# Two feed-forwards with seven block products instead of eight

## The chip, the cores and the metric

The kernel runs on one core of a Trainium2 chip, as one launch. What counts is the device time of that launch in microseconds (us). A core has five engines that run their own queues in order: TensorE (PE, matmuls; its weight loads are listed as PEld), VectorE (DVE), ScalarE (ACT), GpSimd (POOL) and SyncE (SP, which here issues DMAs). They meet through semaphores. Operands lie in SBUF, matmul results in PSUM, which has eight banks of 128 x 512 words.

## The reference, cut to what matters

Two models of two layers each run one after the other on 512 tokens of 1024 features in float32. The first model's two layers end in the feed-forward that the change touches:

```python
def _swiglu(h, w_gate, w_up, w_down):
    return (jax.nn.silu(h @ w_gate) * (h @ w_up)) @ w_down
...
    h = h + _swiglu(_rmsnorm(h, norm_ffn[layer]), w_gate[layer], w_up[layer], w_down[layer])
```

`w_gate` and `w_up` are 1024 x 2816, `w_down` is 2816 x 1024. In slices of 128 that is 8 input slices and 22 hidden ones (`KT`, `FT`).

## The kernel before, in words

Activations are kept transposed: features on the 128 partitions, the 512 tokens along the row. A float32 product is made of three matmuls in the fp32r type: each operand is split into a high part (a rounded copy, made by ACT) and a low part (the value less its high part, made by DVE), and `mm3` adds high x high, low x high and high x low in PSUM. Weights are the stationary operand, so each matmul of 512 columns loads another 128 x 128 weight tile.

Weights arrive in blocks of up to 128 x 1024 words (`wst`, one block for one output slice of 128 and up to eight input slices). `plan` lists all blocks in the order of use, and `w_dma` (L242) fetches them through SP into three buffers. `w_hi` (L274) makes a block's high part `whi` on ACT, `w_lo` (L288) its low part `wlo` on DVE; there are three pairs of `whi` and `wlo` in these parts of the kernel. `cols` (L328) runs one block: 24 matmuls into one bank, then `w_done` (L313) frees the pair, starts the high part of the block three ahead, evacuates the bank and makes that block's low part. The program's order on each engine is the order in which the code calls it; nothing reorders it.

`swiglu` (L1009) takes the 22 hidden slices in three chunks (`CHUNKS`: 8, 7, 7). For each slice it runs gate and up over the eight input slices; DVE scales the bank by the norm's factor `r_bc` (L1018, L1026), ACT applies silu (L1019), DVE multiplies (L1027), and `split_act` (L508) makes the high and low parts `hh`, `hl`. Then down adds the chunk to `x`, slice by slice (`add_res`, L770). The first three blocks run before the norm's factor is known (`first_cols`, L353). With the last chunk each finished slice of `x` is also prepared for the next part (`rms_prep`, L529: high and low part, and POOL adds the squares, L527). In these feed-forwards POOL does little else. The second feed-forward is the same code on the second layer.

## Time and profile before

| what | us |
|---|---|
| median of 3 runs (2577.56 to 2585.64) | 2585.27 |
| the profiled execution | 2584.21 |
| its span, first to last instruction | 2582.3 |
| PE busy in the span | 2533.5 |
| DVE busy in the span | 1557.3 |
| POOL busy in the span | 443.6 |

The profile is one execution. A stretch is given as its two ends, counted in us from the span's start. In the rows below, a timeline gives start, duration, engine, line of the kernel, operation, tile written <- tiles read, shapes and how many were merged, with the idle time before it in brackets. A stretch gives its length, then for PE, PEld, DVE, ACT and POOL the busy time with the number of instructions, then the granted clock of PE as a share of full speed (1.00 is 2.4 GHz, half of it 1.2 GHz), the busy share of the DMA engines and GB/s. A group gives its count, busy time and the mean of one in ns, then the idle time before. Durations of matmuls overlap, since PE takes the next while the last one drains; what one matmul costs is read from start to start.

### The profile page before, as it was taken

To read this page: it belongs to the slowest core of one execution; us is meant where nothing else is said; L and a number is where in the kernel's file an instruction comes from. 1 tells how busy PE (TensorE), PEld (TensorE's weight loads), DVE (VectorE), ACT (ScalarE), POOL (GpSimd) and SP (SyncE) were. 2 spreads that over 40 slices of the span, in tenths; PEclk is the share of its full clock that TensorE was granted. 3 is DMA by queue.
4 is the path that set the end of the run, shared out by engine and by line. 5 is a ranking of instruction groups with operands and counts; after the bars stand their busy time and mean duration, and the time that the engine had idled before them with its cause. 6 is when DMAs were issued, how large, how long until landed. Compare 5 with 4: busy or idle time off the path is not lost.

```text
span 2582.3 us, 32942 instructions
## 1 busy us (share of the span) xinstructions
PE 2533.5 (98%) x12732; PEld 2097.1 (81%) x12732; DVE 1557.3 (60%) x2580; ACT 1045.8 (40%) x1736; POOL 443.6 (17%) x394
## 2 busy tenths in 40 slices
PE   9999999999999999999999999999999999999998
PEld 7777888888767788888888888788888777888887
DVE  7665643444767654444476667764556788745556
ACT  6666422223344442222333333443333574534243
POOL 2112100001545210000111124200102326100103
PEclk9999999999989999999999999899999999999998
DMA  4111222232312122222221112232322312232321
GB/s 146 51 49 48 92 98 98 89 102 96 103 58 77 62 96 92 98 98 99 98 95 58 66 37 78 82 113 92 98 97 83 107 50 74 93 103 88 100 93 55
DMA packets 71277, 220.19 MB, mean 85 GB/s; under 512 B 8741, under 2 KB 15013, under 8 KB 71120
## 3 DMA queue, kind: packets, MB, share of 16 engines
q1 hardware_dynamic: 70512, 216.57, 25.5%
q8 instruction: 100, 1.64, 0.3%
q0 software_dynamic: 464, 1.27, 0.2%
q14 instruction: 57, 0.47, 0.1%
q10 hardware_dynamic: 144, 0.25, 0.0%
HBM read 209.14 MB, written 5.24 MB: 83 GB/s over the span
## 4 chain that ended last, share of the span: by engine, by line
PE 88%; DVE 8%; ACT 2%; issue 1%; DMA 0%; SPq 0%; POOL 0%; DVEq 0%; ACTq 0%
PE bank L225 87%; DVE wlo L295 1%; DVE lt L640 1%; DVE pr L1548 1%; PE bank L1165 1%; ACT whi L286 1%; DVE pr L1157 0%; DVE pr L1535 0%; DVE ln_sm L545 0%; DVE hg L1265 0%; PE bank L1558 0%; DVE hq L1342 0%; DVE xl L653 0%; DMA x<-in_xT 0%; DVE sm L1538 0%
## 5 line engine op out<-in xcount | busy, mean ns | idle before, releaser
L286 ACT ACTIVATE whi<-wst 128x1024 fp32r<-128x1024 f32 (+2 forms) x410 | 411.1, 1008 | 936.5 <-PE bank L225 750.1
L225 PE MATMUL bank<-xh,whi 128*128 128x512 f32 (+1 forms) x1992 | 780.9, 392 | 7.3 <-DVE xh L650 4.8
L225 PE MATMUL bank<-xl,whi 128*128 128x512 f32 (+1 forms) x1992 | 773.5, 388 | 5.0 <-DVE xl L653 2.7
L225 PE MATMUL bank<-xh,wlo 128*128 128x512 f32 (+1 forms) x1992 | 770.5, 387 | 2.3 <-DVE wlo L295 2.3
L295 DVE TENSOR_TENSOR wlo<-wst,whi 128x1024 fp32r<-128x1024 f32 (+2 forms) x392 | 486.4, 1246 | 100.9 <-ACT whi L286 97.4
L225 PEld LDWEIGHTS bank<-xh,whi 128*128 128x128 f32 x1992 | 379.9, 191 | 90.3 <-issue 14.8
L225 PEld LDWEIGHTS bank<-xl,whi 128*128 128x128 f32 x1992 | 379.0, 190 | 85.8 <-DVE xl L653 6.8
L225 PEld LDWEIGHTS bank<-xh,wlo 128*128 128x128 f32 x1992 | 379.9, 191 | 74.4 <-DVE wlo L295 3.7
L225 PE MATMUL bank<-hh,whi 128*128 128x512 f32 (+1 forms) x760 | 285.4, 375 | 0.0
L225 PE MATMUL bank<-hl,whi 128*128 128x512 f32 (+1 forms) x760 | 284.2, 374 | 0.0
L225 PE MATMUL bank<-hh,wlo 128*128 128x512 f32 (+1 forms) x760 | 284.2, 374 | 0.0
L527 POOL TENSOR_TENSOR acc<-acc,sq 128x512 f32<-128x512 f32 x35 | 50.0, 1428 | 789.6 <-ACT sq L526 789.2
L770 DVE TENSOR_TENSOR x<-x,bank 128x512 f32<-128x512 f32 x96 | 65.9, 688 | 187.4 <-PE bank L225 187.4
L225 PEld LDWEIGHTS bank<-hh,wlo 128*128 128x128 f32 x760 | 143.2, 188 | 25.7 <-issue 0.5
L225 PEld LDWEIGHTS bank<-hh,whi 128*128 128x128 f32 x760 | 143.2, 188 | 25.7 <-issue 0.5
L225 PEld LDWEIGHTS bank<-hl,whi 128*128 128x128 f32 x760 | 143.2, 188 | 25.2
L574 POOL TENSOR_TENSOR x<-x,r_bc 128x512 f32<-128x512 f32 x32 | 46.5, 1462 | 480.4 <-ACT r_bc L572 419.9
L225 PE MATMUL bank<-whi,xh 128*128 128x256 f32 x416 | 122.0, 293 | 0.0
L225 PE MATMUL bank<-wlo,xh 128*128 128x256 f32 x416 | 119.5, 287 | 0.0
L225 PE MATMUL bank<-whi,xl 128*128 128x256 f32 x416 | 119.5, 287 | 0.0
L1410 DVE SCALAR_TENSOR_TENSOR b<-bank,vecs,b 128x511 f32<-128x511 f32 x88 | 65.9, 749 | 85.8 <-ACT b L1408 84.2
L1410 DVE SCALAR_TENSOR_TENSOR a<-bank,vecs,a 128x511 f32<-128x511 f32 x88 | 65.9, 749 | 83.8 <-ACT a L1408 82.2
(285 smaller groups left out, 3537.2 us busy)
## 6 DMA issues: line engine op xcount, KB each, us to landing
wst<-in_w SPq DMA_DIRECT2D x314, 512.0 KB, 3.2
wst<-in_w SPq DMA_DIRECT2D x64, 448.0 KB, 3.1
wst<-in_w SPq DMA_DIRECT2D x36, 256.0 KB, 2.7
t<-t SPq DMA_DIRECT2D x56, 64.0 KB, 2.0
rel_scratch<-sq SPq DMA_DIRECT2D x16, 192.0 KB, 2.1
x<-in_xT SPq DMA_DIRECT2D x8, 256.0 KB, 6.2
bias<-rel_scratch SPq DMA_DIRECT2D x16, 128.0 KB, 2.9
out_dram<-x SPq DMA_DIRECT2D x16, 128.0 KB, 1.8
```

The source lines that it names most:

```text
L225: self.nc.tensor.matmul(out, lhsT=l, rhs=r, start=start, stop=True, skip_group_check=True)
L286: self.nc.scalar.activation(out=self.split[i][0][:, 0:n], in_=self.staged[i][:, 0:n], func=AF.Copy)
L295: (eng or self.lo_eng or self.nc.vector).tensor_tensor(out=lo[:, 0:n], in0=st[:, 0:n], in1=hi[:, 0:n].bitcast(F32), op=ALU.subtract)
L527: self.defer(lambda: eng.tensor_tensor(out=self.acc, in0=self.acc, in1=sq, op=ALU.add))
L574: nc.gpsimd.tensor_tensor(out=self.x[:, j, :], in0=self.x[:, j, :], in1=self.r_bc, op=ALU.subtract)
L640: nc.vector.scalar_tensor_tensor(out=t, in0=self.x[:, m, cs], scalar=gm, in1=self.acc[:, cs], op0=ALU.mult, op1=ALU.mult)
L770: self.nc.vector.tensor_tensor(out=self.x[:, m, :], in0=self.x[:, m, :], in1=bank, op=ALU.add)
L1165: nc.tensor.transpose(bk[:, P * j:P * j + P], pr[h][:, P * j:P * j + P], self.ident)
L1410: nc.vector.scalar_tensor_tensor(out=t[:, sh:S], in0=bank[:, 0:S - sh], scalar=self.vec(f"cw{l}{tap}", f), in1=t[:, sh:S], op0=ALU.mult, o ...
L1548: nc.vector.tensor_scalar(out=pr[h][:, 0:W], in0=pr[h][:, 0:W], scalar1=sm[:, 4 + h:5 + h], scalar2=None, op0=ALU.mult)
```

## The change

In both feed-forwards the products of gate, up and down are computed on two by two blocks: for a pair of output slices and pairs of input slices, A is the weights' four quarters (output slice by even or odd input slice), B the activations' four (even or odd input slice by half of the tokens). Seven products of sums replace the eight of the plain rule; each has 256 columns (half of the tokens). Gate and up do so for 9 of the 11 pairs of hidden slices; the first two pairs (`PLAIN`) stay as they were. Down does so for all, in chunks of 4, 4 and 3 pairs (`PCHUNKS`).

Left sides: `S1` to `S4` are sums of weight quarters, made on POOL (`s_adds`) when the same sum of the group before has been read; `w_hi` and `w_lo` then split each of the seven left sides in a piece of 512 (384 in the last chunk), two pieces to a pair of buffers. A fourth weight buffer is added. Right sides: `T1` to `T4` are sums of quarters of the activations. For gate and up they are made once per feed-forward from the normalised `x` (`normed`, `sides_a`, `sides_b`, `sides_in_place`) while the plain slices run; for down once for each pair of hidden slices (`make_h`). Out of PSUM come four sums (`b1`, `b6`, `b7`, `b5`); `seven` combines them through `U` and `V`, and `ev_gate`, `ev_up`, `ev_down` finish each quarter. The product of gate and up, and the sum into `x` in the first two chunks, move to POOL. `down` of a chunk runs between gate and up of the next chunk's first pair.

```diff
+PCHUNKS = ((0, 4), (4, 8), (8, 11))
+PLAIN = 2
+
+PIECES = ("S1", "A11", "S3", "S2", "A12", "A22", "S4")
...
+def swiglu_order():
+    out, done = [], None
+    for c in PCHUNKS:
+        for j in range(max(c[0], PLAIN), c[1]):
+            out.append(("gate", j))
+            if done:
+                out.append(("down", done))
+                done = None
+            out.append(("up", j))
+        done = c
+    return out + [("down", done)]
...
+    def group(w, c, k0, n):
+        for m in (2 * c, 2 * c + 1):
+            out.append((w, [(k, m) for b in (0, 1) for k in range(k0 + b, k0 + n, 2)], None, m == 2 * c))
...
-            self.staged[i] = self.ring.tile([P, 1024], F32, name="wst", bufs=3)
+            self.staged[i] = self.stages.pop(0)
...
+            i = self.n_dma - 2
+            if i >= 0 and self.blocks[i][3] and not (i >= 2 and self.blocks[i - 2][3]):
+                self.s_adds(i, ("S1", "S2", "S3", "S4"))
...
+    def s_adds(self, i, names):
+        how = {"S1": ("A21", "A22", ALU.add), "S2": ("S1", "A11", ALU.subtract), "S3": ("A11", "A21", ALU.subtract),
+               "S4": ("A12", "S2", ALU.subtract)}
+        for n in names:
+            a, b, op = how[n]
+            self.nc.gpsimd.tensor_tensor(out=self.side(i, n), in0=self.side(i, a), in1=self.side(i, b), op=op)
...
+            for h, (i, name) in enumerate(load):
+                src = self.side(i, name)
+                c = slice(512 * h, 512 * h + src.shape[-1])
+                self.nc.vector.tensor_tensor(out=lo[:, c], in0=src, in1=hi[:, c].bitcast(F32), op=ALU.subtract)
+                more = i + 2 < len(self.blocks) and self.blocks[i + 2][3]
+                if more and name in ("S1", "S2", "S4"):
+                    self.s_adds(i + 2, {"S1": ("S1",), "S2": ("S2", "S3"), "S4": ("S4",)}[name])
+                if name in ("A12", "A22"):
+                    self.stages.append(self.staged.pop(i + int(name[1]) - 1))
+                    self.w_fetch()
...
+    def seven(self, name, nk, act, banks, evac):
+        x, y = banks
+        b1, b6, b7, b5 = x[:, 0:256], x[:, 256:512], y[:, 0:256], y[:, 256:512]
+        uv = self.uv.tile([P, 2, 256], F32, name="uv", bufs=2)
+        U, V = uv[:, 0, :], uv[:, 1, :]
+        tt = self.nc.vector.tensor_tensor
+        steps = (
+            ("S1", "T1", b5, True, None),
+            ("A11", "B11", b1, True, lambda: self.nc.scalar.activation(out=U, in_=b1, func=AF.Copy)),
+            ("S3", "T3", b7, False, None),
+            ("S2", "T2", b6, False, lambda: (tt(out=U, in0=b6, in1=U, op=ALU.add), tt(out=V, in0=b7, in1=U, op=ALU.add),
+                                             evac(1, 1, b5, V))),
+            ("A12", "B21", b1, False, lambda: evac(0, 0, b1, None)),
+            ("A22", "T4", b7, False, lambda: evac(1, 0, b7, U)),
+            ("S4", "B22", b5, False, lambda: evac(0, 1, b5, U)),
+        )
+        for side, other, out, start, then in steps:
+            load = self.loads[self.wi]
+            i, n = load[self.half]
+            assert n == side and self.blocks[i][0] == name and self.wi < self.n_lo, (load, side, name)
+            hi, lo = (t[:, 512 * self.half:512 * self.half + 512] for t in self.split[self.wi])
+            for k in range(nk):
+                c = slice(k * P, (k + 1) * P)
+                self.mm3(out, hi[:, c], lo[:, c], act(other, 0, k), act(other, 1, k), start and k == 0)
+            self.half += 1
+            full = self.half == len(load)
+            if full:
+                self.half = 0
+                self.wi += 1
+                self.w_free()
+                self.w_hi()
+            if then:
+                then()
+            if full:
+                self.w_lo()
+            self.flush()
...
+            def make_h(j):
+                b11, b12, b21, b22 = b[:, 0, 0:256], b[:, 0, 256:S], b[:, 1, 0:256], b[:, 1, 256:S]
+                rows = (slice(0, 1), slice(1, 3), slice(3, 7))
+                src = (b[:, 0:1, 0:256], b[:, 1, :].rearrange("p (a c) -> p a c", a=2), t4)
+                hi = lambda n: nc.scalar.activation(out=h[j][0][:, rows[n], :], in_=src[n], func=AF.Copy)
+                lo = lambda n: ve(out=h[j][1][:, rows[n], :], in0=src[n], in1=h[j][0][:, rows[n], :].bitcast(F32), op=ALU.subtract)
+                hi(0)
+                hi(1)
+                ve(out=t4[:, 0], in0=b12, in1=b11, op=ALU.subtract)
+                ve(out=t4[:, 2], in0=b22, in1=b12, op=ALU.subtract)
+                ve(out=t4[:, 1], in0=b22, in1=t4[:, 0], op=ALU.subtract)
+                ve(out=t4[:, 3], in0=b21, in1=t4[:, 1], op=ALU.subtract)
+                hi(2)
+                lo(0)
+                lo(1)
+                self.defer(lambda: lo(2))
...
+            def normed(k):
+                v = (even, odd)[k % 2][:, k // 2, :]
+                nc.vector.scalar_tensor_tensor(out=v, in0=self.x[:, k, :], scalar=self.vec(f"norm_ffn{l}", k), in1=self.r_bc,
+                                               op0=ALU.mult, op1=ALU.mult)
+            def side_x(n, src):
+                out = [quad(t[:, n, :, :]) for t in tx]
+                nc.scalar.activation(out=out[0], in_=src, func=AF.Copy)
+                self.defer(lambda: ve(out=out[1], in0=src, in1=out[0].bitcast(F32), op=ALU.subtract))
+            def sides_a():
+                gp(out=t1, in0=quad(x12), in1=quad(x11), op=ALU.subtract)
+                side_x(0, t1)
+                gp(out=t3, in0=quad(x22), in1=quad(x12), op=ALU.subtract)
+                side_x(2, t3)
+            def sides_b():
+                t2 = quad(t4)
+                gp(out=t2, in0=quad(x22), in1=t1, op=ALU.subtract)
+                side_x(1, t2)
                 self.flush()
-
-            def ev_u(i):
-                def f(bank):
-                    b = pool.tile([P, S], F32, name="b", bufs=2)
-                    nc.vector.tensor_tensor(out=b, in0=bank, in1=self.r_bc, op=ALU.mult)
-                    nc.vector.tensor_tensor(out=b, in0=b, in1=hold["a"], op=ALU.mult)
-                    self.split_act(h, i, b)
+                gp(out=t1, in0=quad(x21), in1=t2, op=ALU.subtract)
+                side_x(3, t1)
...
+            def sides_in_place():
+                for m, c, src in ((0, 0, x11), (1, 0, x21), (1, 256, x22)):
+                    hi, lo = (t[:, m:KT:2, c:c + 256] for t in self.xn)
+                    nc.scalar.activation(out=hi, in_=src, func=AF.Copy)
+                    ve(out=lo, in0=src, in1=hi.bitcast(F32), op=ALU.subtract)
+            extra = [lambda k=k: (normed(2 * k), normed(2 * k + 1)) for k in range(4)] + [sides_a, sides_b]
+            names = [(f"{n}{l}", e) for f in range(2 * PLAIN) for n, e in (("gate", ev_g(f % 2)), ("up", ev_u(f)))]
+            run(self.first_cols([n for n, _ in names[:3]], self.xn, [lin.next() for _ in range(3)], [e for _, e in names[:3]]))
+            todo = {3: extra[0:2], 4: extra[2:4], 5: extra[4:5], 6: extra[5:6]}
+            for n, (name, e) in enumerate(names[3:], 3):
+                for f in todo.get(n, ()):
+                    f()
+                run(self.cols(name, range(KT), self.xn, lin.next(), e))
+            self.flush()
+            sides_in_place()
+            pre_cm.__exit__(None, None, None)
+            post_cm = self.tc.tile_pool(name="post", bufs=1)
+            h += sides_of_pairs(post_cm.__enter__(), (2, 3))
...
+            def ev_up(j):
+                def f(m, n, bank, more):
+                    c = slice(256 * n, 256 * n + 256)
+                    if more is None:
+                        ve(out=b[:, m, c], in0=bank, in1=a[:, m, c], op=ALU.mult)
+                        return
+                    ve(out=b[:, m, c], in0=bank, in1=more, op=ALU.add)
+                    if (m, n) == (1, 0):
+                        gp(out=b[:, 1, :], in0=b[:, 1, :], in1=a[:, 1, :], op=ALU.mult)
+                    if (m, n) == (0, 1):
+                        gp(out=b[:, 0, c], in0=b[:, 0, c], in1=a[:, 0, c], op=ALU.mult)
+                        self.defer(lambda: make_h(j))
                 return f
 
...
+                    t = pool.tile([P, 256], F32, name="t", bufs=2)
+                    ve(out=t, in0=bank, in1=more, op=ALU.add)
+                    eng(out=x, in0=x, in1=t, op=ALU.add)
...
+            for what, j in swiglu_order():
+                if what == "gate":
+                    self.seven(f"gate{l}", 4, act_x, pairs.next(), ev_gate)
+                elif what == "up":
+                    self.seven(f"up{l}", 4, act_x, pairs.next(), ev_up(j % 4))
+                else:
+                    self.flush()
+                    for m in range(4):
+                        self.seven(f"down{l}", j[1] - j[0], act_h, pairs.next(), ev_down(m, j is PCHUNKS[-1]))
```

What stands on DVE in the first feed-forward, before: three blocks of weights (`wlo`), each with the evacuation of one bank (`a` gate, `b` up) and its split (`hl`).

```order
L1026 TENSOR_TENSOR b<-bank_73,r_bc 128x512
L1027 TENSOR_TENSOR b<-b,a 128x512
L295 TENSOR_TENSOR wlo_100<-wst,whi_99 128x1024
L1018 TENSOR_TENSOR a<-bank_74,r_bc 128x512
L514 TENSOR_TENSOR hl<-b,hh 128x512
L295 TENSOR_TENSOR wlo_102<-wst,whi_101 128x1024
```

Now, in the second half of one `up` and the start of the next `gate`: `S_2550` to `S_2553` are S1 to S4, `wst` the weight buffers, `t_2549` the four sums T of a pair, `uv` holds U and V.

```order
L382 TENSOR_TENSOR wlo_102<-S_2552,whi_101 128x512
L382 TENSOR_TENSOR wlo_102<-S_2551,whi_101 128x512
L1282 TENSOR_TENSOR b<-bank_79,uv 128x256 x2
L382 TENSOR_TENSOR wlo_98<-wst_2554,whi_97 128x512
L382 TENSOR_TENSOR wlo_98<-wst_105,whi_97 128x512
L1187 TENSOR_TENSOR t_2549<-b 128x256
L1188 TENSOR_TENSOR t_2549<-b 128x256
L1189 TENSOR_TENSOR t_2549<-b,t_2549 128x256
L1190 TENSOR_TENSOR t_2549<-b,t_2549 128x256
L1184 TENSOR_TENSOR hl_2884<-b,hh_2883 128x256
L1184 TENSOR_TENSOR hl_2884<-b,hh_2883 128x512
L1184 TENSOR_TENSOR hl_2884<-t_2549,hh_2883 128x1024
```

Where there was one `wlo` of 1024 for 24 matmuls of 512 columns there are now two of 512 for 24 matmuls of 256, with sums of 256 out of two banks between them and the seven right sides of the pair at its end.

POOL before, around the start of the first feed-forward: the last sums of the attention, then sums of squares (`acc`), most of them from the end of the feed-forward, and the first gain of the next part's weights.

```order
L971 TENSOR_TENSOR spl_2168<-sp,sph_2167 128x256
L971 TENSOR_TENSOR spl_2171<-sp,sph_2170 128x256
L527 TENSOR_TENSOR acc<-acc,sq 128x512 x10
L267 TENSOR_TENSOR wst<-wst,vecs 128x1024
L527 TENSOR_TENSOR acc<-acc,sq 128x512
```

POOL now, in the steady part of gate and up: the four sums of each group's weights, and the product of gate and up in two pieces.

```order
L349 TENSOR_TENSOR S_2550<-wst_104 128x512
L349 TENSOR_TENSOR S_2551<-S_2550,wst_103 128x512
L349 TENSOR_TENSOR S_2552<-wst_103,wst_104 128x512
L1284 TENSOR_TENSOR b<-b,a 128x512
L1286 TENSOR_TENSOR b<-b,a 128x256
L349 TENSOR_TENSOR S_2553<-wst_103,S_2551 128x512
L349 TENSOR_TENSOR S_2550<-wst_105 128x512
L349 TENSOR_TENSOR S_2551<-S_2550,wst_2554 128x512
```

Between two products there are eight sums of 512, where POOL had nothing at all.

DVE before, where slices of gate and up follow each other, as everywhere in the chunk:

```order
L295 TENSOR_TENSOR wlo_98<-wst,whi_97 128x1024
L1018 TENSOR_TENSOR a<-bank_76,r_bc 128x512
L514 TENSOR_TENSOR hl<-b,hh 128x512
L295 TENSOR_TENSOR wlo_100<-wst,whi_99 128x1024
L1026 TENSOR_TENSOR b<-bank_77,r_bc 128x512
L1027 TENSOR_TENSOR b<-b,a 128x512
```

DVE now, from the evacuation of the last plain `up` to the normalised low parts `xl` that the second of the seven products reads:

```order
L1207 TENSOR_TENSOR b<-bank_73,r_bc 128x512
L1208 TENSOR_TENSOR b<-b,a 128x512
L1187 TENSOR_TENSOR t_2549<-b 128x256
L1188 TENSOR_TENSOR t_2549<-b 128x256
L1189 TENSOR_TENSOR t_2549<-b,t_2549 128x256
L1190 TENSOR_TENSOR t_2549<-b,t_2549 128x256
L1184 TENSOR_TENSOR hl_2544<-b,hh_2543 128x256
L1184 TENSOR_TENSOR hl_2544<-b,hh_2543 128x512
L382 TENSOR_TENSOR wlo_100<-wst_2554,whi_99 128x512
L382 TENSOR_TENSOR wlo_100<-wst_105,whi_99 128x512
L1184 TENSOR_TENSOR hl_2544<-t_2549,hh_2543 128x1024
L1249 TENSOR_TENSOR xl<-even,xh 128x4x256
```

The evacuation of the last plain slice, the seven right sides of its pair and two pieces of weights stand ahead of `xl`.

## Rows read from the trace of the kernel before

**Rows 1.** The page, busy time of each engine
```profile
PE 2533.5 (98%) x12732; PEld 2097.1 (81%) x12732; DVE 1557.3 (60%) x2580; ACT 1045.8 (40%) x1736; POOL 443.6 (17%) x394
```

**Rows 2.** The page, chain that ended last, by engine
```profile
PE 88%; DVE 8%; ACT 2%; issue 1%; DMA 0%; SPq 0%; POOL 0%; DVEq 0%; ACTq 0%
```

**Rows 3.** Stretches: both feed-forwards, and one around a pause of PE
```profile
core 0: us, PE busy (x) PEld busy (x) DVE busy (x) ACT busy (x) POOL busy (x), PEclk, DMA share, GB/s
292.50:653.00 360.50, 360.48 (x1598) 298.82 (x1599) 159.95 (x202) 105.00 (x130) 16.59 (x11) 1.00 0.29 96
934.80:1295.00 360.20, 360.17 (x1597) 298.62 (x1598) 160.16 (x202) 105.66 (x130) 10.03 (x7) 1.00 0.29 96
706.00:722.00 16.00, 11.25 (x30) 7.29 (x29) 11.96 (x22) 5.41 (x12) 5.24 (x4) 0.68 0.21 69
```

**Rows 4.** Timeline of PE: start, duration; 512 columns, first feed-forward
```profile
399.91 0.39 PE L225 MATMUL bank<-hh,whi 128*128 128x512 f32 x1
...
410.79 0.39 PE L225 MATMUL bank<-hh,whi 128*128 128x512 f32 x1
```

**Rows 5.** Timeline of PE, 256 columns, each with another weight tile
```profile
206.84 0.28 PE L225 MATMUL bank<-whi,xl 128*128 128x256 f32 x1
...
212.35 0.28 PE L225 MATMUL bank<-wlo,xh 128*128 128x256 f32 x1
```

**Rows 6.** Timeline of DVE and POOL, runs of one instruction merged, at 13 us
```profile
13.57 6.87 DVE L517 SCALAR_TENSOR_TENSOR xl<-x,vecs,xh 128x512 fp32r<-128x512 f32 x4
...
13.48 10.34 POOL L527 TENSOR_TENSOR acc<-acc,sq 128x512 f32<-128x512 f32 x6 [0.39 <-ACT sq L526]
```

**Rows 7.** Timeline of DVE and POOL, two places where both run
```profile
637.45 1.90 POOL L267 TENSOR_TENSOR wst<-wst,vecs 128x1024 f32<-128x1024 f32 x1
...
638.79 0.69 DVE L770 TENSOR_TENSOR x<-x,bank 128x512 f32<-128x512 f32 x1 [2.47 <-PE bank L225]
...
1630.32 0.77 POOL L646 TENSOR_TENSOR x<-lt,acc 128x256 f32<-128x256 f32 x1 [0.95 <-ACT r_bc L641]
...
1630.42 1.75 DVE L295 TENSOR_TENSOR wlo<-wst,whi 128x1024 fp32r<-128x1024 f32 x1
```

**Rows 8.** Timeline of DVE, instructions without a wait between them
```profile
639.39 0.69 DVE L514 TENSOR_TENSOR xl<-x,xh 128x512 fp32r<-128x512 f32 x1
...
1606.82 0.42 DVE L579 TENSOR_TENSOR x<-x,bank 128x256 f32<-128x256 f32 x1 [0.19 <-PE bank L225]
...
1607.16 0.42 DVE L594 TENSOR_TENSOR acc<-acc,sq 128x256 f32<-128x256 f32 x1
```

**Rows 9.** Groups by line, shapes apart: DVE, ACT, POOL; busy us, mean ns
```profile
L295 DVE TENSOR_TENSOR wlo<-wst,whi 128x1024 fp32r<-128x1024 f32 x52 | 63.3, 1221 | 12.7 <-ACT whi L286 12.5
...
L295 DVE TENSOR_TENSOR wlo<-wst,whi 128x512 fp32r<-128x512 f32 x24 | 16.7, 702 | 3.8 <-ACT whi L286 3.7
...
L653 DVE TENSOR_TENSOR xl<-x,xh 128x256 fp32r<-128x256 f32 x48 | 19.5, 417 | 3.2 <-ACT xh L652 3.2
...
L946 DVE TENSOR_TENSOR spl<-sp,sph 128x384 fp32r<-128x384 f32 x32 | 17.9, 559 | 2.1
...
L1276 DVE SCALAR_TENSOR_TENSOR x<-x,vecs,r_bc 128x512 f32<-128x512 f32 x8 | 5.4, 747 | 0.0
...
L579 DVE TENSOR_TENSOR x<-x,bank 128x256 f32<-128x256 f32 x40 | 16.4, 413 | 10.1 <-PE bank L225 8.7 <-POOL acc L591 1.4
...
L286 ACT ACTIVATE whi<-wst 128x1024 fp32r<-128x1024 f32 x314 | 331.0, 1058 | 735.0 <-PE bank L225 579.7 <-issue 142.9 <-POOL wst L267 4.5
...
L286 ACT ACTIVATE whi<-wst 128x512 fp32r<-128x512 f32 x32 | 19.9, 626 | 37.6 <-PE bank L225 34.3 <-issue 2.2 <-ACT pr L1149 1.1
...
L295 POOL TENSOR_TENSOR wlo<-wst,whi 128x1024 fp32r<-128x1024 f32 x10 | 23.9, 2395 | 2.7 <-ACT whi L286 2.5
...
L591 POOL TENSOR_TENSOR acc<-acc,x 128x256 f32<-128x256 f32 x39 | 30.5, 781 | 42.3 <-DVE x L579 35.2 <-DVE ln_sm L545 5.5 <-DVE acc L594 0.7
```

**Rows 10.** The page, DMA issues of weight blocks
```profile
wst<-in_w SPq DMA_DIRECT2D x314, 512.0 KB, 3.2
```

202 lines of the change are left out of this document (144 added, 58 removed).

## Prediction

> **What bounds the kernel now.** I read the shares of busy time first, then the chain that ended last, then the two feed-forwards as stretches, then what VectorE (DVE) and GpSimd (POOL) do to each other, because the change hands both of them work. TensorE (PE) is busy 98% of the span, DVE 60%, POOL 17% [rows 1], and PE carries 88% of the chain [rows 2]. Each of the two feed-forwards is a stretch of 360 us in which PE is busy throughout at full clock, DVE 160 us and POOL 10 to 17 us [rows 3]. So before, PE alone sets the pace there, and the question is whether the change leaves it so.
>
> **What it does to PE.** From one matmul of 512 columns to the next there are 0.2267 us: 48 steps between the two rows of [rows 4]. With 256 columns and a fresh weight tile for each it is 0.1198 us, 46 steps in [rows 5]. Half the columns cost 53% of the time, so seven products cost 7 x 2 x 0.53 / 16 of the eight: most of the eighth is kept. Per feed-forward the change replaces 864 matmuls of gate and up (9 pairs of slices x 96) and 528 of down, 1392 x 0.2267 = 315.6 us, by 9 x 168 + 4 x 11 x 21 = 2436 of 256 columns, 291.8 us. That is 23.8 us less, 47.6 us in both. It is the whole gain.
>
> By the page TensorE: Matmul & The Clock Gate of the Trainium skill (Back-to-back issue gap), a stream of weight load and matmul sustains about 131 ns at 512 columns and about 81 ns at 128; 256 columns then lie between, some 98 ns as an estimate, and 84 x 98 ns against 48 x 131 ns would make seven products dearer than eight. The trace has 227 and 120 ns where the page has 131 and its estimate 98, so I keep the gain.
>
> **What it costs DVE and POOL in steady state.** Take one pair of slices, gate and up: PE needs 168 x 0.1198 = 20.1 us, before 96 x 0.2267 = 21.8.
> DVE issues an instruction 0.61 us after one of 512 the starts at 638.79 and 639.39 in [rows 7, 8], 0.34 after one of 256 [rows 8], 1.14 after one of 1024 (its 1.22 less the same 0.08). Per pair it gets 14 low parts of 512 (8.5 us), 11 sums or products of 256 that read PSUM (3.7), four sums for T1 to T4 each waiting for the one before (4 x 0.42 = 1.7, taken at a full 256-wide duration, [rows 9]) and the low parts of the seven right sides (0.34 + 0.61 + 1.14 = 2.1): 16.0 us, which would fit.
> POOL gets 8 sums of weight quarters of 512 and two products, of 512 and 256. They are not free for DVE. At 13.5 us both had such work queued: six POOL sums took 10.34 us and four DVE instructions 6.87 us, 1.72 us each [rows 6], so they took turns; alone the DVE one takes 0.61, and a POOL 512 thus holds DVE up for 1.11 us. A 1024-wide DVE instruction with 256 of POOL ahead of it took 1.75 instead of 1.22 us [rows 7, 9], so 0.6 for a POOL 256. A DVE instruction with one operand in PSUM is not held: 0.69 us in the middle of a POOL instruction of 1.90 [rows 7].
> So POOL's holds are 9 x 1.11 + 0.6 = 10.6 us a pair. If every one falls on a DVE instruction with both operands in SBUF, the pair takes 16.0 + 10.6 = 26.6 us; if the 3.7 us of PSUM reading always run beneath POOL, 22.9. Either is above PE's 20.1 and above the 21.8 of before: the lower end holds unless POOL's work falls into time in which DVE has nothing to do, and there is none left once DVE is behind. I take 23.4, near the lower end, as both queues are then hardly ever empty, with half a microsecond for DVE's waits on its own results and on POOL's product. Nine pairs: +1.6 x 9 = +15 us a feed-forward (bounds +10, +44). ScalarE (ACT) has 14 x 0.63 us for high parts plus some 4 us [rows 9], well under 20: nothing.
>
> By the page SBUF — State Buffer of the Trainium skill (Who interferes with whom), whichever of the two comes first keeps the shared port for its whole instruction; a POOL 512 would then hold 1.28 us and a pair take 24.5. The trace's turns of 1.72 us leave 1.11, which decides.
>
> **Down.** A group over four pairs has 84 matmuls, 10.1 us, before 48 and 10.9. DVE 7 x 0.61 + 6 x 0.34 = 6.3, POOL 4 x 1.11 + 3 x 0.6 = 6.2; 12.5 together, 10.5 if the six PSUM readers are covered. I take 10.8: eight groups, -1 us (bounds -3, +13). The last groups cover three pairs: PE 7.6 us, before 36 x 0.2267 = 8.2. DVE has 7 low parts of 384 (0.56 less 0.08 each, [rows 9], 3.4), nine of 256 (3.1) and two low parts of x (1.4): 7.9; POOL 4 x 0.85 plus two sums of squares 2.2: 5.6. Together 13.5, covered 11.5; the last group has no next one to prepare, some 9. I take 10.7 for three and 9: +8 for the four (bounds -2, +18).
>
> **Two places where PE is left standing.** (1) From the plain slices to the first seven. Between the third block and the first normalised low part `xl` DVE is given 33 us: eight PSUM reads of 512 (4.9), four products (2.4), three weight parts of 1024 (3.4), eight `normed` of 0.67 (5.4; 0.75 less 0.08, [rows 9]), `make_h` twice (7.6), six weight parts of 512 (3.7), four `tl` (4.6) and the first `xl` (1.1). POOL is given eight sums of 512 (8.9) and four of 1024 (2.40 each, [rows 9], so 2.2 of hold: 8.8). PE has five blocks and the first product for it, 28.6 us, and no other work, since the second product needs that `xl`. 33 + 17.7 - 4.9 covered + 1 us of late start - 28.6 = 18 us of pause; without any hold 6, with every hold 23. Some of POOL's first sums can run while DVE still waits for the first results, so I take 13. A pause costs clock as well: after one of 3.6 us from 707 the granted clock over 706 to 722 was 0.68, thus the lower level for about 10 us [rows 3]. As PE then waits for DVE anyway, I count 2 us of it (0 to 7).
> (2) The last down follows straight on the last up: 0.34 for the sum, POOL's 0.8, the four sums 1.7, the high part of 1024 1.06 and its low part 1.14, after two weight parts, 1.2, less 0.7 of product on the other two pairs: 5 us (3 to 8). In the other chunks the next gate covers this, and before, the last slice came as the last of seven in down.
> Weights: the same bytes at a DMA share of 0.29 [rows 3], 3.2 us to land [rows 10], in four buffers for three; SP issues a block when its buffer is read, a group ahead: nothing; a late block would cost up to its 3.2 us each. The last sums into x are halves and end beneath the next part's first blocks: nothing.
>
> **Sum.** Per feed-forward +15 - 1 + 8 + 13 + 2 + 5 = +42 us, all against the time of before, so with PE's 24 us already in it; twice, +84. The profiled execution took 2584.2 us (span 2582.3, 1.9 around it), 1 us under the median 2585.3: 2584 + 84 = 2668 us. With all lower ends (10 - 3 - 2 + 6 + 0 + 3 = 14) it is 2612, with all upper ends (44 + 13 + 18 + 23 + 7 + 8 = 113) 2810.
>
> **Rivals.** (a) PE still sets the pace: POOL's instructions fall into DVE's idle time, and a pair takes its 20.1 us. For it: DVE alone needs 16.0 of 20.1, and the stretch at 13.5 us is a crowd that need not be typical. Against it: 16.0 + 10.6 - 3.7 leaves no idle time. Gain 47.6, less 2 x (6 + 3) at the two places: 2555 us. Faster begins where a pair takes under about 21. (b) A draw: the pair lands at 21.5 and the pauses at their lower ends, so that the gain pays for them: 2585. (c) The holds cost in full, and the pauses leave the clock at its lower level for long: 2790 or more. For it: one POOL instruction after a DVE weight part is always ready when the next DVE part starts; against: the eleven PSUM readers a pair. (d) The change does not do what it says: 256 columns with new weights run slower than 0.12 us where both operands change each time. Against: in [rows 5] the weights change each time too. From 0.1296 us (315.6 / 2436) on nothing is gained; there, with the lower ends of the two places, 2584 + 18 = 2602.
>
> **How the numbers follow.** Forecast (DVE and POOL in turns set the pace) 0.68; (a) 0.16; (b) 0.06; (c) 0.07; (d) 0.03. A difference under 0.3%, 8 us, can't be told from none. Faster: (a) and a little of (b), 0.17; same 0.06; slower, forecast, (c), (d), 0.77. The forecast's own range is 2612 to 2750; down to 2570 it takes in (b) and the near edge of (a). Left out are most of (a) below and (c) above.
>
> **What would show it.** Right: in the feed-forwards DVE is busy 85% or more, its low parts of 512 average about 1 us instead of 0.7 while POOL's sums average over 1.4, PE's idle time before matmuls is ended by DVE `wlo`, a pair takes 23 to 24 us from gate to gate, and PE pauses some 13 us after the plain slices with the clock falling behind it. Wrong: PE without gaps, pairs of 20 us, low parts of 0.7 us beside POOL's sums; or low parts held up but their lead over PE never used up, the holds then being paid for by waiting time. If the pairs are as said and the pause is not, the sum is 30 us lower.

## The result, and the profile after

The changed kernel takes 2809.9 us (median of 4 runs, 2806.6 to 2815.3), the kernel before 2584.7 beside it: a ratio of 1.088, 95% interval 1.085 to 1.091. The forecast had the direction and a third of the size: +84 us, and it is +225. The time lies above the forecast's own range (2612 to 2750), at the upper end of all its bounds added up (2810), but not by the terms that it had there.

The page after: busy time of each engine, and the chain that ended last.

```profile
PE 2577.7 (92%) x14820; PEld 2213.9 (79%) x14820; DVE 1911.6 (68%) x3230; ACT 1221.8 (44%) x2150; POOL 899.4 (32%) x726
...
PE 71%; DVE 17%; issue 4%; POOL 3%; ACT 3%; DMA 0%; SPq 0%; ACTq 0%; DVEq 0%; POOLq 0%
```

PE's share of the chain fell from 88% to 71% and DVE's rose from 8% to 17% [rows 1, 2]. That is what the forecast wanted to see; the next view is not. Stretches of the first feed-forward after, to be held against [rows 3]: most of the pairs with two downs; ten us behind one wait of PE; the step from the plain slices to the first seven; the whole.

```profile
395.00:690.00 295.00, 244.36 (x1838) 233.53 (x1838) 203.04 (x325) 121.98 (x217) 167.88 (x125) 0.93 0.26 78
521.00:531.00 10.00, 8.41 (x36) 7.83 (x36) 4.54 (x9) 2.90 (x7) 2.83 (x2) 0.50 0.02 5
330.00:365.00 35.00, 18.86 (x79) 15.81 (x78) 28.85 (x29) 15.06 (x22) 16.57 (x9) 0.71 0.14 45
292.50:766.00 473.50, 380.32 (x2630) 355.44 (x2631) 334.73 (x523) 191.78 (x335) 241.69 (x176) 0.91 0.24 73
```

The feed-forward that ended at 653 now ends past 766. DVE, the fourth column, is busy 203 of 295 us, 69%, and POOL 57%: neither sets the pace alone, as 85% or more would have said of DVE. PE stands still a sixth of the time and its clock is not at full speed. So somebody waits for somebody in a ring. What PE waited for in the same feed-forward (total us, times, longest):

```profile
PE bank L261 <- ACT uv L505: 28.3, 11, 3.2
PE bank L261 <- DVE uv L507: 25.0, 30, 4.7
PE bank L261 <- ACT hh L1183: 12.7, 2, 8.3
PE bank L261 <- DVE t L1299: 8.5, 11, 1.4
PE bank L261 <- DVE b L1282: 5.6, 9, 0.6
PE bank L261 <- DVE a L1270: 4.7, 9, 0.5
PE bank L261 <- DVE wlo L376: 3.3, 1, 3.3
```

The forecast expected `wlo` here, the low parts of the weights. It ends one wait of 3.3 us. Two more, 12.7 us before `hh`, belong to the two places where PE was expected to stand. The other five rows, 72 us, are readers of PSUM: the copy of b1 into U (L505), the sums into U and V (L507), and the sums of the banks with U or V into t, b and a. PE, timeline rows with a wait, 17 us from one gate into a down group:

```profile
420.03 0.38 PE L261 MATMUL bank<-th,whi 128*128 128x256 f32 x1 [3.20 <-ACT uv L505]
422.30 0.38 PE L261 MATMUL bank<-xh,whi 128*128 128x256 f32 x1 [0.59 <-DVE uv L507]
425.93 0.39 PE L261 MATMUL bank<-xh,whi 128*128 128x256 f32 x1 [0.52 <-DVE a L1270]
433.80 0.39 PE L261 MATMUL bank<-hh,whi 128*128 128x256 f32 x1 [0.52 <-DVE uv L507]
```

These waits are built into the program. `seven` puts b1 and b6 into the two halves of one bank and b7 and b5 into those of another, and PE is made to wait before it writes one half until the reader of the other half is through: S2·T2, which goes to b6, waits for ScalarE's copy of b1. By the Trainium skill, page PSUM — Partial Sum Buffer (PSUM bank collisions raise a hardware error), a matmul and another engine's read must not be in one bank and the same 32 partitions at once, disjoint columns or not, so that access has to be ordered by bank rather than by address. The trace agrees in that the waits are there and take 0.5 to 0.6 us even where the reader has nothing ahead of it; what happens without them no run here shows.

The 3.20 us have another part. The timeline before that matmul, of DVE, POOL and ACT, with PE's last matmul into b1 (415.13):

```profile
412.94 2.46 DVE L382 TENSOR_TENSOR wlo<-wst,whi 128x512 fp32r<-128x512 f32 x2
...
414.81 1.19 POOL L1286 TENSOR_TENSOR b<-b,a 128x256 f32<-128x256 f32 x1
...
415.13 0.28 PE L261 MATMUL bank<-xl,whi 128*128 128x256 f32 x1
...
416.02 0.43 DVE L1187 TENSOR_TENSOR t<-b 128x256 f32<-128x256 f32 x1 [0.63 <-POOL b L1286]
...
417.16 0.42 DVE L1190 TENSOR_TENSOR t<-b,t 128x256 f32<-128x256 f32 x1
...
417.61 1.06 ACT L1183 ACTIVATE hh<-t 128x1024 fp32r<-128x1024 f32 x1 [2.10 <-DVE t L1190]
418.58 1.13 ACT L365 ACTIVATE whi<-S 128x512 fp32r<-128x512 f32 x2
...
419.62 0.36 ACT L505 ACTIVATE uv<-bank 128x256 f32<-128x256 f32 x1
```

ScalarE's instructions run in the order in which they were issued, and the copy of b1 stands behind the high part of the T sums (`hh<-t`), which waits for DVE's four sums, which wait for POOL's product b·a. The product in its turn stands in POOL's queue behind two sums of weights: its first piece began at 413.11, 2.3 us after the last sum that it reads (410.40, 0.42 long). The last matmul into b1 ended at 415.4; its copy began 4.2 us later. Eight of the nine pairs have this wait, always 3.2 us, and behind six of the eight the granted clock was at its lower level, 1.2 GHz, for 3 to 10 us (0.50 from 521 to 531, above). The "nothing" that the forecast put down for ScalarE was true of its busy time and not of its queue.

### The profile page after: what moved, and what is told of

Same layout as the page of the kernel before. It is cut to its first block, busy times and chain, and to the rows that moved or that the text cites. A ratio compares the mean times of both kernels' runs of the same rounds, so it can differ in the third digit from the quotient of the medians.

```text
span 2808.3 us, 39052 instructions
## 1 busy us (share of the span) xinstructions
PE 2577.7 (92%) x14820; PEld 2213.9 (79%) x14820; DVE 1911.6 (68%) x3230; ACT 1221.8 (44%) x2150; POOL 899.4 (32%) x726
## 3 DMA queue, kind: packets, MB, share of 16 engines
q1 hardware_dynamic: 70512, 216.57, 24.9%
## 4 chain that ended last, share of the span: by engine, by line
PE 71%; DVE 17%; issue 4%; POOL 3%; ACT 3%; DMA 0%; SPq 0%; ACTq 0%; DVEq 0%; POOLq 0%
PE bank L261 70%; DVE wlo L382 3%; DVE wlo L376 2%; POOL S L349 1%; DVE uv L507 1%; ACT whi L365 1%; POOL b L1284 1%; DVE lt L773 1%; ACT whi L361 1%; POOL b L1286 1%; DVE pr L1817 1%; PE bank L1434 1%; DVE hl L1184 0%; DVE t L1299 0%; DVE t L1187 0%
## 5 line engine op out<-in xcount | busy, mean ns | idle before, releaser
L261 PE MATMUL bank<-xh,whi 128*128 128x512 f32 (+1 forms) x1848 | 694.1, 376 | 55.2 <-DVE uv L507 21.8
L376 DVE TENSOR_TENSOR wlo<-wst,whi 128x1024 fp32r<-128x1024 f32 (+2 forms) x272 | 349.1, 1289 | 91.1 <-ACT whi L361 89.7
L261 PE MATMUL bank<-hh,whi 128*128 128x256 f32 (+1 forms) x1024 | 331.3, 324 | 59.5 <-DVE uv L507 26.3
L261 PE MATMUL bank<-hl,whi 128*128 128x256 f32 (+1 forms) x1024 | 323.8, 316 | 0.9 <-DVE hl L1184 0.9
L261 PE MATMUL bank<-hh,wlo 128*128 128x256 f32 (+1 forms) x1024 | 323.7, 316 | 0.0
L261 PE MATMUL bank<-th,whi 128*128 128x256 f32 x576 | 177.3, 308 | 68.0 <-ACT uv L505 51.3
L365 ACT ACTIVATE whi<-S 128x512 fp32r<-128x512 f32 (+1 forms) x240 | 145.0, 612 | 175.0 <-PE bank L261 161.7
L382 DVE TENSOR_TENSOR wlo<-S,whi 128x512 fp32r<-128x512 f32 (+1 forms) x240 | 185.0, 788 | 28.9 <-ACT whi L365 28.0
L382 DVE TENSOR_TENSOR wlo<-wst,whi 128x512 fp32r<-128x512 f32 (+1 forms) x180 | 166.4, 937 | 23.5 <-ACT whi L365 22.9
L261 PE MATMUL bank<-th,wlo 128*128 128x256 f32 x576 | 173.9, 302 | 0.0
L261 PE MATMUL bank<-tl,whi 128*128 128x256 f32 x576 | 173.8, 302 | 0.0
```

Source lines behind the costliest of these rows:

```text
L261: self.nc.tensor.matmul(out, lhsT=l, rhs=r, start=start, stop=True, skip_group_check=True)
L365: self.nc.scalar.activation(out=room[0][:, 512 * h:512 * h + src.shape[-1]], in_=src, func=AF.Copy)
L376: (eng or self.lo_eng or self.nc.vector).tensor_tensor(out=lo[:, 0:n], in0=st[:, 0:n], in1=hi[:, 0:n].bitcast(F32), op=ALU.subtract)
L382: self.nc.vector.tensor_tensor(out=lo[:, c], in0=src, in1=hi[:, c].bitcast(F32), op=ALU.subtract)
```

## The experiments

Theory A is the forecast's: GpSimd holds VectorE up, and the two in turns set the pace. Theory B came from the trace above: banks shared by two sums, and queues in which a reader of PSUM stands behind somebody else's wait. The yardstick beside the time is the stretch from the first sum `a` of the first gate to that of the ninth, first feed-forward: eight pairs and eight down groups, after 692.60 - 366.60 = 326.0 us:

```profile
366.60 0.42 DVE L1270 TENSOR_TENSOR a<-bank,uv 128x256 f32<-128x256 f32 x1
...
692.60 0.42 DVE L1270 TENSOR_TENSOR a<-bank,uv 128x256 f32<-128x256 f32 x1
```

The forecast's sizes give 8 x 23.4 + 8 x 10.8 = 273.6, PE alone 8 x 20.1 + 8 x 10.1 = 241.6. All kernels are compared with the kernel before by runs on the same chip, where that took 2577.2 to 2584.7 us; two kernels that lie close are therefore compared by their ratios. "Stretch" is that of the first feed-forward, "pair" the mean distance of two gates with no down between them, in both.

| kernel | us | ratio, interval | stretch | pair |
|---|---|---|---|---|
| changed kernel | 2809.9 | 1.085-1.091 | 326.0 | 29.0 |
| bank for each sum | 2717.6 | 1.051-1.055 | 285.9 | 25.2 |
| T high part two steps later | 2811.4 | 1.088-1.091 | 324.5 | 28.4 |
| small sums on POOL | 2754.5 | 1.064-1.069 | 306.4 | 26.6 |
| products on VectorE | 2776.3 | 1.074-1.078 | 315.2 | 27.2 |
| T part four steps later | 2827.4 | 1.093-1.098 | 330.1 | 29.1 |
| bank each, T four later | 2742.6 | 1.062-1.065 | 294.6 | 25.5 |
| the same, small sums | 2630.3 | 1.018-1.021 | 250.5 | 21.3 |
| the same (whole sums), x sides first | 2731.3 | 1.056-1.061 | 295.5 | 25.2 |
| bank each, small sums | 2623.7 | 1.015-1.019 | 249.1 | 21.2 |
| bank each, small sums, idle POOL work | 2688.7 | 1.041-1.045 | 273.3 | 23.7 |
| bank each, all on VectorE | 2803.5 | 1.085-1.090 | 323.5 | 26.9 |
| the same, S1 later | 2707.1 | 1.048-1.052 | 280.1 | 24.6 |
| bank each, products on VectorE, x sides first | 2694.3 | 1.042-1.047 | 279.0 | 23.9 |

**A bank for each sum**

```diff
-        x, y = banks
-        b1, b6, b7, b5 = x[:, 0:256], x[:, 256:512], y[:, 0:256], y[:, 256:512]
+        b1, b6, b7, b5 = (t[:, 0:256] for t in banks)
...
-            ("S3", "T3", b7, False, None),
+            ("S3", "T3", b7, True, None),
...
-        pairs = Ring([(self.bank[2 * i], self.bank[2 * i + 1]) for i in range(4)])
+        pairs = Ring([self.bank[4 * i:4 * i + 4] for i in range(2)])
```

> Each of the four sums of a product (b1, b6, b7, b5) gets a PSUM bank of its own instead of half of a shared one; nothing else is changed. Theory B (the sums that share a bank make TensorE wait for the ScalarE or VectorE instruction that reads the other half, and the lower clock follows): in the first feed-forward TensorE's waits of 0.5 to 0.8 us inside a product go (some 50 us), the wait of 3.2 us after each up shrinks by the 1.4 us of one step, the clock stays up more; about -75 us a feed-forward, 2660 us in all. Theory A (VectorE and GpSimd in turns set the pace): their work is the same, so the pair of slices keeps its 28 to 30 us and the time stays above 2790 us.

92 us gone, of 150 that B forecast and at most 20 that A allowed: 40 us of each feed-forward's stretch. What PE waited for from 395 to 690, and the busy times there:

```profile
PE bank L261 <- ACT uv L504: 22.8, 8, 3.5
PE bank L261 <- ACT hh L1182: 5.2, 1, 5.2
PE bank L261 <- DVE uv L506: 4.1, 6, 1.0
```
```profile
395.00:690.00 295.00, 260.86 (x2043) 255.87 (x2041) 255.44 (x372) 137.49 (x249) 190.85 (x140) 0.94 0.28 86
```

The `hh` row belongs to the last down, which begins earlier here. The short waits inside gate and up are gone. The long one is not shorter (2.8 to 3.5 us in seven of the eight), only one step later, at A12·B21, which adds to b1 itself. B had expected 1.4 us less of it. But from the end of the last sum of b to the copy of b1 it now takes 7.8 us (498.29 to 506.07) where it took 6.6 (413.03 to 419.62): the product, behind two sums in POOL's queue, starts 1.7 us after that sum instead of 0.1. And now DVE is busy 255 of 295 us, 87%: what the forecast had described begins here.

**T high part two steps later; T part four steps later**

The edit of the first of the two; in the second the four T sums are put off with the high and the low part:

```diff
-                hi(2)
                 lo(0)
                 lo(1)
-                self.defer(lambda: lo(2))
+                self.defer(lambda: self.defer(lambda: (hi(2), lo(2))))
```

> ScalarE's high part of the four T sums (hh from t4, 1024 columns) and VectorE's low part of it are issued two steps later, behind the next product's copy of b1, so that this copy no longer stands behind an instruction that waits for GpSimd's product. Banks stay shared. Theory B: the wait of 3.2 us before S2-T2 of each gate falls under 1 us and the lower clock behind it goes: 8 places a feed-forward, 2 us each, and up to 18 us of clock, 2740 us in all. Theory A: VectorE and GpSimd have the same work, so within 10 us of 2810.

> In every pair that is made by seven products, all of the T part (VectorE's four T sums, ScalarE's high part, VectorE's low part) is issued four steps later, behind the next product's U and V sums, so that neither ScalarE's queue nor VectorE's holds that product's sums up behind GpSimd's product. Banks stay shared. Theory B: the one wait of 3.2 us per pair falls to the 0.5 to 0.8 us of the other products, and the clock stays up: 8 places, 2.5 us each, and 12 us of clock, -32 us a feed-forward, 2745 us. Theory A (VectorE and GpSimd in turns set the pace): the same work in another order, 2800 us.

(In the first of the two the plain pairs' T part is put off as well, and is taken after t4 is written anew; this part of the computation is changed.) Both missed: no gain, and with four steps 18 us lost. The longest wait of each, once per pair:

```profile
423.81 0.58 PE L261 MATMUL bank<-xh,whi 128*128 128x256 f32 x1 [3.76 <-DVE uv L507]
```
```profile
397.26 0.58 PE L261 MATMUL bank<-xh,whi 128*128 128x256 f32 x1 [4.26 <-DVE a L1281]
```

ScalarE's copy came in time, and PE then stood at the next reader: with the high and low part moved, at VectorE's sum into U, behind the low part of the T sums (2.28 us long there); with all of it moved, at the sum of b7 into a, behind the same low part. In both, the wait that was put off in an in-order queue went to whoever was issued next. B was right on who waits, wrong that this one cut would pay.

**Small sums, and the products on VectorE (banks shared)**

```diff
-            self.nc.gpsimd.tensor_tensor(out=self.side(i, n), in0=self.side(i, a), in1=self.side(i, b), op=op)
+            self.nc.gpsimd.tensor_tensor(out=self.side(i, n)[:, 0:8], in0=self.side(i, a)[:, 0:8], in1=self.side(i, b)[:, 0:8], op=op)
```
```diff
-                        gp(out=b[:, 1, :], in0=b[:, 1, :], in1=a[:, 1, :], op=ALU.mult)
+                        ve(out=b[:, 1, :], in0=b[:, 1, :], in1=a[:, 1, :], op=ALU.mult)
...
```

> GpSimd's sums S1 to S4 of the weight quarters are taken over 8 columns of 512 only (so the output leaves out most of them; the rest of their tiles is zero). Everything else, waits included, is as in the changed kernel. This takes nearly all of GpSimd's work beside VectorE away. Theory A: the pair falls from 28-30 us to TensorE's 20 us, down groups with it; 2640 us or less. Theory B: VectorE's low parts get shorter (0.69 us instead of 0.94), which shortens the waits that VectorE ends but neither the shared banks nor the copy behind the T sums: 2740 to 2790 us.

> The product b times a of both parts goes from GpSimd to VectorE. Theory B: the four T sums start about 0.8 us earlier, so ScalarE's copy of b1 behind them too; 8 places a feed-forward, 0.8 us each, and some of the clock: 2780 to 2800 us. Theory A: GpSimd's holds of 1.7 us a pair turn into 0.95 us of VectorE work: 9 pairs twice, 13 us, 2795 us; the two differ only in the length of the wait before S2-T2 of the gate (B: 2.4 us instead of 3.2; A: the same).

Small sums took 55 us away, B's range and not A's 170. The products took 34, more than either had: the wait before S2·T2 fell from 3.20 to 2.15 us (2.4 expected), and the granted clock from 395 to 690 was 0.95 after 0.93.

```profile
390.69 0.39 PE L261 MATMUL bank<-th,whi 128*128 128x256 f32 x1 [2.15 <-ACT uv L505]
```

**Bank each, with the T part later, with small sums, with the x sides first**

> Both edits: a bank for each sum, and the T part four steps later. Theory B: the waits of 2.8 to 3.5 us before A12-B21 of each gate go with their clock, no wait of TensorE over 1 us is left inside the pairs, and a pair takes 20.5 to 22 us: 2640 us. Theory A: with TensorE's own waits gone, VectorE beside GpSimd sets the pace, at the 23.4 us a pair of the forecast: 2670 us, VectorE over 90% busy, and TensorE's waits are ended by VectorE's low parts of the weights (wlo).

> Both edits, and GpSimd's sums S1 to S4 over 8 columns of 512 only (the output leaves out most of them). It prices GpSimd's holds on VectorE once TensorE no longer waits for shared banks or the T part. Theory A: a pair falls from 23.4 to TensorE's 20.1 us, and down groups by some 0.7: 40 us a feed-forward with its clock, 2600 us or less. Theory B: TensorE sets the pace either way, within 15 us of the kernel with both edits.

> Both edits, and at the step from the plain slices to the first seven the sides of x that are written in place (x11, x21, x22) are issued ahead of the seven sides of h of the second plain pair, not behind them. Both theories: TensorE's pause there, 12.7 us before xh and some 5 us around it, falls to 5 us or less, and the 20 us of lower clock behind it to 7: 12 to 17 us a feed-forward, 24 to 34 us under the kernel with both edits.

With both edits it is 25 us slower than with the banks alone; both theories had expected a gain. The T part now comes among the weight parts of the next gate, and the next product's U and V sums come late in their place. DVE and then PE, with both edits:

```profile
497.35 1.75 DVE L382 TENSOR_TENSOR wlo<-wst,whi 128x512 fp32r<-128x512 f32 x1
499.03 0.87 DVE L506 TENSOR_TENSOR uv<-bank,uv 128x256 f32<-128x256 f32 x2
```
```profile
499.95 0.38 PE L261 MATMUL bank<-th,whi 128*128 128x256 f32 x1 [2.81 <-DVE uv L506]
```

Here a `wlo` that took 1.75 instead of 0.68 us stands ahead of what PE waits for, while POOL makes a sum (496.97 to 498.55). With small sums the same kernel is 112 us faster, its pair 21.3 instead of 25.5 us, and its low parts of S and of the quarters take 722 and 807 ns instead of 900 and 1307. That is A's mechanism, priced far above B's 15 us. The third kernel issues `sides_in_place` ahead of `make_h` for the second plain pair; it gave 11 us over the kernel with both edits, not 24 to 34: the wait for xh went from 12.8 to 5.9 us, but the one for xl behind it rose from 1.6 to 3.9 and the clock stayed low as long.

**Bank each with small sums; with POOL busy at nothing; with all on VectorE**

> A bank for each sum, the T part at its old place, and GpSimd's sums S1 to S4 over 8 columns of 512 only (the output leaves out most of them). Theory C (once the banks are apart, GpSimd's holds on VectorE set the pace, 25.2 us a pair where TensorE needs 20.1): the pair falls to 21 to 22 us and down groups by 0.7, 35 to 40 us a feed-forward, 2640 us. Rival (the wait of 2.8 to 3.5 us behind the T part sets the pace by itself, and that is GpSimd's product, which stays): pairs of 24 us or more, 2690 us.

> A bank for each sum, and all of GpSimd's sums in the feed-forwards (S1 to S4, the products b times a, the sums into x) done by VectorE. Nothing is left out. Theory C: VectorE's own work in a pair rises from 16.0 to 16.0 + 8 x 0.61 + 0.95 = 21.9 us, but 10.6 us of holds go: pairs of 22 to 23 us, VectorE over 95% busy, 2650 to 2670 us. Rival: holds cost VectorE little (they fall into its waits), so that 5.9 us more work makes the pair longer than its 25.2 us: 2730 us or more.

> As the kernel with everything on VectorE, and at the step from the plain slices to the first seven the sides written in place come ahead of the sides of h of the second plain pair. It gave 5.6 us a feed-forward beside the late T part; the same here: 11 us under the kernel with everything on VectorE. Theory C says nothing else of it.

> As the kernel with everything on VectorE, and ScalarE's high part and VectorE's low part of the four T sums two steps later, behind the next product's copy of b1. Theory C (VectorE's work sets the pace): the same work, within 8 us of the kernel with everything on VectorE. Rival (ScalarE's copy of b1 behind the T part still stops TensorE once per pair): 1 to 2 us a pair less, 20 to 35 us under it.

Small sums fit theory C and went past it: 94 us gone, pairs of 21.2. All on VectorE did not: 2803.5 us, 86 more than with POOL, in the rival's range. Both variants of it missed all that was expected of them and changed nothing for the better (2805.8 with the x sides first, and 2816.9 with the T part later). What DVE waited for from 395 to 690:

```profile
DVE S L349 <- DMA wst<-in_w: 36.4, 15, 3.2
```

S1 is issued as soon as its buffer is free, when its weight block has not landed. In POOL's queue the sums waited for the same (11.6 us in nine waits with the banks alone); in DVE's queue such a wait holds up all that PE needs from it. So this run said nothing of the holds, and two more were made for them, the first on the kernel with small sums, the second on the one with all on VectorE:

```diff
+        for n in names:
+            self.nc.gpsimd.tensor_tensor(out=self.idle, in0=self.r_bc[:, 0:448], in1=self.r_bc[:, 0:448], op=ALU.add)
```
```diff
-                if more and name in ("S1", "S2", "S4"):
-                    self.s_adds(i + 2, {"S1": ("S1",), "S2": ("S2", "S3"), "S4": ("S4",)}[name])
+                if more and name in ("S2", "S4"):
+                    self.s_adds(i + 2, {"S2": ("S1", "S2", "S3"), "S4": ("S4",)}[name])
```

> As the kernel with a bank for each sum and GpSimd's sums over 8 columns (the output leaves out most of them), and behind each small sum GpSimd does one more TENSOR_TENSOR of 448 columns, on two SBUF operands that nobody writes, into a tile that nobody reads. So GpSimd is as busy as with the whole sums, but no one waits for that work. Holds (GpSimd's instructions stop VectorE's): the low parts of 512 go from 0.72-0.79 back to 0.9-1.15 us, the pair from 21.2 to 24-25 us, 2690 to 2710 us. Latency (what counted was the time until a sum was there, for ScalarE's and VectorE's next step): the pair stays under 22 us, 2625 to 2645 us.

> As the kernel with everything on VectorE, but S1 of the group after next is issued with S2 and S3, two low parts later, so that VectorE no longer stands at it until the weight block has landed (36 us of such waits in 295). Nothing is left out. Theory C (VectorE's work, 21.9 us a pair, against 16.0 plus 10.6 of holds with GpSimd): pairs of 22 to 23 us, 2650 to 2690 us. Rival (holds fall into VectorE's waits, so that more work of its own only adds): 25 us a pair or more, 2717 us or above.

POOL work whose result nobody reads costs 65 us (2623.7 to 2688.7), 69% of what the whole sums cost, and it lengthens VectorE's low parts (groups below). How much of the 65 us is VectorE being held this run does not show: the idle work also stands in POOL's queue ahead of the product b·a, and for that VectorE waits. POOL in the run with idle work, where the product's last operand was there at 490.08; then what VectorE waited for from 395 to 690, with idle work and with whole sums:

```profile
490.20 2.27 POOL L351 TENSOR_TENSOR idle<-r_bc 128x448 f32<-128x448 f32 x2
492.44 1.74 POOL L1288 TENSOR_TENSOR b<-b,a 128x512 f32<-128x512 f32 x1
```
```profile
DVE t L1191 <- POOL b L1290: 13.8, 8, 1.9
```
```profile
DVE t L1186 <- POOL b L1285: 12.6, 8, 1.9
```

With small sums the product starts 0.1 us after its operand (477.11 to 477.23), and VectorE does not wait for it. So small sums took two things away, the holds and a queue of some 2.5 us ahead of the product, and here too the copy of b1 came late behind it: PE's waits for that copy are 20.7 us with idle work, 22.8 with whole sums and 4.9 with small ones. The kernel with the T part four steps later separates the two better. In it VectorE waits for POOL nowhere from 395 to 690, and small sums still take 4.2 us off its pair; but ScalarE's wait for the product goes with them there (18.3 us to 2.2), so that this too is not the holds alone. Groups by line, 395 to 690, the low parts of the weights: with small sums, with the idle POOL work, with whole sums.

```profile
L382 DVE TENSOR_TENSOR wlo<-S,whi 128x512 fp32r<-128x512 f32 x85 | 60.7, 731 | 11.1 <-ACT whi L365 11.1
L382 DVE TENSOR_TENSOR wlo<-wst,whi 128x512 fp32r<-128x512 f32 x65 | 52.1, 815 | 11.9 <-ACT whi L365 11.9
```
```profile
L384 DVE TENSOR_TENSOR wlo<-S,whi 128x512 fp32r<-128x512 f32 x88 | 72.5, 848 | 2.9 <-ACT whi L367 2.9
L384 DVE TENSOR_TENSOR wlo<-wst,whi 128x512 fp32r<-128x512 f32 x66 | 70.9, 1088 | 10.2 <-ACT whi L367 9.9
```
```profile
L382 DVE TENSOR_TENSOR wlo<-wst,whi 128x512 fp32r<-128x512 f32 x68 | 84.5, 1255 | 10.5 <-ACT whi L365 10.5
L382 DVE TENSOR_TENSOR wlo<-S,whi 128x512 fp32r<-128x512 f32 x89 | 82.9, 954 | 0.9 <-ACT whi L365 0.6
```

A pair has eight low parts of S and six of the quarters: 8 x (954 - 731) + 6 x (1255 - 815) ns = 4.4 us that the low parts lost to the eight sums, half of the 8 x 1.11 = 8.9 that the forecast had. The pair grew by 4.0; what part of that comes from the holds and what from the queue ahead of the product is open. With the sums on VectorE and no wait for the weights the kernel takes 2707.1 us, a ratio of 1.050 where the one with the banks alone has 1.053, with intervals that overlap: no clear gain. The low parts are back at 0.68 us, but the pair is 24.6: theory C's 22 to 23 did not come, nor the rival's 2717 or more.

**Three cuts together**

> A bank for each sum, the products b times a on VectorE, and at the step from the plain slices to the first seven the sides written in place ahead of the sides of h of the second plain pair. Nothing is left out; GpSimd keeps S1 to S4 and the sums into x. On shared banks the products gave 33 us, and the other order 11 us beside the late T part. Each of the three cuts another wait, so they add: 2670 to 2680 us. If VectorE's holds are what is left of the pair (25.2 us), the products give no more than 9 x 0.75 x 2 = 13 us: 2690 to 2700 us.

2694.3 us, the bounded case: products and x sides give 23 us together where on other ground they gave 34 and 11. It is the fastest kernel here that leaves nothing out, 4.5% (4.2 to 4.7) over the kernel before. Even with nearly all of the weight sums gone (2623.7) it is 1.7% over, so no order of this work that was tried beats it. There the steady part does gain: its stretch is 249.1 us, where the kernel before needs 8 x 21.8 + 8 x 10.9 = 261.6 for the same work. The time is lost at the two ends of each feed-forward, some 33 us each as an estimate: half of the 41.6 us by which this kernel is over, and the 12.5 us that its steady part gains. In the first feed-forward PE waits 11.7 and 1.6 us at the step to the first seven, and up to 6.1 us at a time in the last down.

## Why the prediction was right and wrong

**PE's gain** was right: 256 columns kept their 0.12 us (three steps from 711.25 to 711.61), and with small sums the pair came down to 21.2 us where PE alone needs 20.1. (The share "7 x 2 x 0.53 / 16" is a slip, 7 x 0.53 / 4 = 0.93 is meant; the sum in us does not use it.) Rival (d) fell. **Rival (a)** fell too: the low parts do get longer beside POOL, and no pair of the changed kernel took less than 27.5 us.

**The steady pair is the step that failed:** "I take 23.4, near the lower end, as both queues are then hardly ever empty", between bounds of 22.9 and 26.6. It is 29.0, outside. The bounds were sums of work. They had no term for PE waiting on the readers of its own banks, and ScalarE, whose copy of b1 ends the longest of these waits, was put at "nothing" by its busy time. The shared banks were there to see: the diff puts two sums in one bank, and the order of the instructions shows who reads them. That term is 326.0 - 285.9 = 40.1 us a feed-forward in the stretch, and 92 us of the kernel, of the 142 by which the forecast fell short. The working asked what stands in front of DVE's low parts and never who stands in front of the copy of b1.

With the banks apart the stretch is 285.9, 12 over the forecast's 273.6, and DVE is at 87%, near the forecast's picture, but with two terms wrong in opposite directions. The holds on the low parts were half as dear (4.4 us a pair against 8.9 for the sums, though of all holds the forecast let 3.7 run beneath PSUM readers), and the waits on POOL's product and on ScalarE, taken at half a microsecond, were 3 us of PE each pair. That own-bank sums with idle POOL work give 273.3 is therefore luck and no proof of the 23.4. The 24.5 that the working sets beside the 23.4 leaves out that half microsecond; with it the same sum is 24.9.

**Down groups** over four pairs: 46 us for four by the gates (75.0 - 29.0 from 422.7 to 497.7), 11.5 each for the 10.8 taken; with the banks apart 10.5.

**Place 1** was near on the pause and short on the clock. PE's rows there, next to the 13 us forecast:

```profile
335.70 0.50 PE L261 MATMUL bank<-xh,wlo 128*128 128x512 f32 x1 [3.30 <-DVE wlo L376]
351.13 0.55 PE L261 MATMUL bank<-th,whi 128*128 128x256 f32 x1 [8.32 <-ACT hh L1183]
356.97 0.58 PE L261 MATMUL bank<-xh,whi 128*128 128x256 f32 x1 [2.94 <-ACT xh L1248]
359.35 0.58 PE L261 MATMUL bank<-xl,whi 128*128 128x256 f32 x1 [1.58 <-DVE xl L1249]
```

16.1 us together. The longest stands before the first product and not, as forecast, before the second; with a bank for each sum it does stand there, one wait of 12.7 us before `xh`. The holds weigh less in it than thought: with small sums as well it is still 11.7. The granted clock from 330 to 365 was 0.71, so the lower level for 35 x 0.29 / 0.5 = 20 us, where 10 us, of which 2 would count, were taken.

**Place 2** was right: 4.43 us before the last down's first T for the 5 taken.

```profile
716.55 0.58 PE L261 MATMUL bank<-hh,whi 128*128 128x256 f32 x1 [4.43 <-ACT hh L1183]
```

The last down itself was mis-sized: with that wait it takes 59.5 us from its first matmul to its last in one feed-forward (711.3 to 770.8) and 53.5 in the other, for 5 + 3 x 10.7 + 9 = 46.1. The 10.7 lay below the forecast's own covered sum of 11.5, without a reason; and waits on the readers of banks are in it here too.

**The clock** had 4 us in the forecast. Over 395 to 690 it is 0.93, the lower level for some 40 us of 295. Rival (c), at 2790 or more, had the time, but by "the holds cost in full", and they cost half; its second half, a clock that stays low, was true, through waits of PE that it did not have.

**What would have shown it** named the right views. The low parts (816 and 990 ns from 395 to 690) and POOL's sums (1305 to 1568 ns) came out close to what was expected. But DVE's share (69% and not 85%) and the releaser of PE's waits (`wlo` once) both said that the forecast's mechanism was not the one that set the pace.

## What to carry to other kernels

Before an engine's busy time is added up, list for each PSUM bank who writes and who reads it between two steps, and in whose queue the reader stands behind what: in this kernel two sums in one bank made each reader a wait of the matmul stream. A bound made of work alone is not an upper bound where engines wait for each other in a ring. Moving an operation that waits for data to a faster engine moves its wait into that engine's queue. And work whose result nobody reads is still waited for by whatever stands behind it in the same queue, so it is no clean measure of contention.
